# Weight sums added two pieces behind their loads, weights moved to multiples of 512 bytes, and four sigmoids spread out, in a decoder layer on Trainium2

## The chip, the cores and the metric

The kernel runs as one program on one core of a Trainium2 chip. The metric is the device time of one launch in microseconds (us); less is better. All times below are of that kind or come from one profiled execution of the same program.

The engines are named as in the profile: PE is the matrix engine (PEld is its loading of weights), DVE the vector engine, ACT the scalar engine, POOL the general one, SP the engine whose queue issues nearly all transfers. Each engine works through its own instructions in the order of the program.

## The reference

One decoder layer, in float32, for a sequence of S = 256 tokens of width D = 2048 (two blocks of 128 rows). Three kinds of attention read the same normalised input, gates mix them, and a gated feed-forward part follows:

```python
h = rms_norm(x, g_mix)
fq, fk, fv, f_logit, sq, sk, sv, mq, gates = split(h @ w_in)      # 6 + 6 + 4 heads of 128
o_fox = forgetting_attention(rms(fq), rms(fk), fv, cumsum(log_sigmoid(f_logit + b_forget)))
o_sb  = stick_breaking_attention(sq, sk, sv)
mk, mv = split(rms_norm(mem, g_mem) @ w_mem_kv)
o_mem = memory_attention(rms(mq), rms(mk), mv)
g = sigmoid(gates + b_gate)                                       # three gates, 2048 wide each
x = x + (g0*(o_fox @ w_br_fox) + g1*(o_sb @ w_br_sb) + g2*(o_mem @ w_br_mem)) @ w_out
u = causal_depthwise_conv(rms_norm(x, g_ffn) @ w_up)              # w_up is 2048 x 11264
x = x + (silu(u_gate) * u_val) @ w_down                           # w_down is 5632 x 2048
```

## The kernel before, in words

**Products.** Every float32 operand is split into a part `hi` and a rest `lo`, and each product is three passes: hi by hi, lo by hi, hi by lo (`three`, L284 to L286, and `passes`). Activations are the stationary operand ("weights" of PE), the model's matrices are the moving one, up to 512 columns at a time. `product` walks over the rows of a matrix in pieces of two blocks of 128 rows: a 512 KB load into one of four buffers `raw` (L140, on SP), a copy to `hi` on ACT (L141), a subtraction to `lo` on DVE (L142), both with four buffers, and then 12 matmuls. After each piece it calls `tick()`.

**Seven products for eight.** For parts of the gates, for the output projection and for the down projection, `blocked` replaces some groups of eight block products by seven. This needs sums of blocks of the matrix (`t_g`, `raw_t_d` and so on) and sums of blocks of the activations: `xs` for x (made by `x_sums`), `ms` for the merged heads, `sf` for the feed-forward part. In a gate's plan, such as "esesesee", "s" is a group of seven and "e" one of eight; four gates are done by such plans, with three "s" each.

**Weight sums ahead of time.** For the output and down projections the sums of the matrix are made in the background while the earlier stages run, and are kept in DRAM. `weight_sums` (L243 to L272) is a generator that `tick()` steps once. For one half of a sum it issues two loads of 256 KB (`pre`, L258), three additions on DVE (L265 to L267), and, `store` ticks after the loads, a store of 512 KB (`kept`, L270). After `period` ticks the next half begins. There is one buffer `pre`, so that a load has to wait for the store before it to land. While the first stages run, `period` is 4 and `store` is 3; from the third gate on (once "heads" is in `issued`) the period is 8. What is left at "merged" is done in the feed-forward stage by two further such generators with other buffers. There are 58 halves, 14 of `w_out` and 44 of `w_down`.

**Heads.** The attention heads are generators too, queued by `later` and stepped by `tick()`, at most two at a time: while PE does the projection of the next stage, it does the heads of the one before in between. `fox_head` has its PE work at L820 to L822 (`fa`, `fb`) and L724, after DVE copies at L815 and L837 (`fx`); stick-breaking heads are around L880 to L900.

**Order.** PE, DVE, ACT and SP instructions of the products, sums and loads are held in program order. The stages follow each other as: memory keys and values, memory queries, the fox projections f0 to f4, the stick-breaking projections s0 to s4, gates, branches, output projection, up, down.

**First sigmoids.** The first two gates are made by `product` while the last heads run. Their four sigmoids (two per gate, 128x1024 each) are issued together in `ready`, at the first blocked gate (L984), when the heads are done.

**Addresses.** Tiles of the pools are laid out one after the other in a partition's memory. In the kernel before, `ident` and `xs` stand 384 bytes past a multiple of 512; `xT`, `hi`, `lo`, `raw`, `pre` and nearly all other large tiles stand 32 bytes past one.

Of the kernel before, what the change touches and what calls it, by code (L numbers as in the profile page):

```python
# [9 lines left out]
F32 = mybir.dt.float32  # L10
F32R = mybir.dt.float32r
AF = mybir.ActivationFunctionType
# [3 lines left out]
P = 128  # L16
S = 256
NT = S // P
# [23 lines left out]
def hybrid_block(  # L42
# [25 lines left out]
    nc = tc.nc  # L68
    nc.scalar.preload_act_table_set("natural_log_exp_and_others")

    cst = ctx.enter_context(tc.tile_pool(name="cst", bufs=1))
    wp = ctx.enter_context(tc.tile_pool(name="wp", bufs=WBUFS))
    xt_pool = ctx.enter_context(tc.tile_pool(name="xt_pool", bufs=1))
    sm = ctx.enter_context(tc.tile_pool(name="sm", bufs=4))
    idle = cst.tile([P, 384], mybir.dt.bfloat16, name="idle")
    nc.vector.memset(idle, 0.0)
    sm_pad = sm.tile([P, 160], F32, tag="pad", bufs=1, name="sm_pad")
    nc.gpsimd.memset(sm_pad, 0.0)
# [2 lines left out]
    def bank(name):  # L81
        return pp.tile([P, 512], F32, tag="bank", name=name)
# [3 lines left out]
    spare = bank("spare")  # L86

    def keep_busy(n):
        for _ in range(n):
            tc.keep_in_program_order(  # L90
                nc.tensor.matmul(spare[:, :384], lhsT=idle[:, :P], rhs=idle, start=True, stop=True)
            )


# [2 lines left out]
    def later(gen):  # L97
        waiting.append(gen)
# [24 lines left out]
    def finish():  # L123
        while waiting or active:
            tick(beside=False)
# [104 lines left out]
    in_order = tc.keep_in_program_order  # L230
# [9 lines left out]
        for h in range(2)  # L240
    )

    def weight_sums(staging, period, store, end=None, delay=0, slower=0):  # L243


        for _ in range(delay):
            yield
        while halves and end not in issued:
            name, wv, nb, pr, h = halves.popleft()
            at = f"{name}{nb}_{pr}"  # L250
            if h == 0:
                sums_of[name, nb, pr] = dram.tile([P, 4, 512], F32, tag=f"kept_{at}", name=f"kept_{at}")
            kept = sums_of[name, nb, pr]
            w = staging(f"pre_{at}_{h}").rearrange("p (i c) -> p i c", i=4)
            n0 = nb * PIECE + h * 256
            for n in range(2):
                in_order(
                    nc.sync.dma_start(  # L258
                        w.rearrange("p (k n) c -> p k n c", k=2)[:, :, n],
                        wv[:, 2 * pr : 2 * pr + 2, n0 + n * 512 : n0 + n * 512 + 256],  # L260
                    )
                )

            both = w[:, 1:2].to_broadcast([P, 2, 256])
            in_order(nc.vector.tensor_tensor(w[:, 0:2], w[:, 0:4:3], both, ALU.add))  # L265
            in_order(nc.vector.tensor_tensor(w[:, T2], w[:, T1], w[:, T2], ALU.add))
            in_order(nc.vector.tensor_tensor(w[:, T4], w[:, T2], w[:, T4], ALU.add))  # L267
            for _ in range(store):
                yield
            in_order(nc.sync.dma_start(kept[:, :, h * 256 : (h + 1) * 256], w))  # L270
            for _ in range(period - store + (slower if "heads" in issued else 0)):
                yield  # L272
# [206 lines left out]
    nc.gpsimd.affine_select(  # L479
        after_r, ones, pattern=[[-1, P]], compare_op=ALU.is_gt, fill=0.0, base=0, channel_multiplier=1  # L480
    )
    qscale = cst.tile([P, 1], F32, name="qscale")
    nc.vector.memset(qscale, SCALE)

    keep_busy(7)
# [61 lines left out]
        nc.vector.tensor_reduce(tot, ss, AX.X, ALU.add)  # L547
        rsqrt_mean(dst, tot, NT, D, name)

    rstd = cst.tile([P, NT], F32, name="rstd")  # L550
    rstd_m = cst.tile([P, NT], F32, name="rstd_m")
    rstd_f = cst.tile([P, NT], F32, name="rstd_f")
    ssm = cst.tile([P, NT, 4], F32, name="ssm")
    ssx = cst.tile([P, NT, 4], F32, name="ssx")
    ssf = cst.tile([P, NT, 4], F32, name="ssf")

    rneg = cst.tile([P, NT], F32, name="rneg")

    mix = ctx.enter_context(ExitStack())
    op = mix.enter_context(tc.tile_pool(name="op", bufs=1))  # L560
# [1 line left out]
    gp = mix.enter_context(tc.tile_pool(name="gp", bufs=3))  # L562

    def block(name, dt=F32):
        return bp.tile([P, 1024], dt, tag="blk", name=name)
# [4 lines left out]
    def rows_of(b):  # L570
        return b.rearrange("p (t n) -> p t n", t=NT)
# [85 lines left out]
    def kv_tiles(k):  # L657
        return [
            wp.tile([P, PIECE], dt, tag=tag, bufs=n, name=f"{tag}_kv{k}")
            for tag, dt, n in (("raw", F32, WBUFS), ("hi", F32R, SBUFS), ("lo", F32R, SBUFS))  # L660
        ]

    tiles = kv_tiles(0)
# [56 lines left out]
    def weighted(pT, v, h, oh, o):  # L720
# [7 lines left out]

    ps = proj(C_MQ, MEM_W, "mq")
    background.append(  # L730
        weight_sums(lambda name: gp.tile([P, 1024], F32, tag="pre", bufs=1, name=name), 4, 3, "merged", slower=4)
    )
    finish()
    qm = heads_of(block("qm"))
# [204 lines left out]
    def merged_sums():  # L939
        yield 1  # L940
        for p in range(o_plans[0].count("s")):
            ms[p] = block(f"ms_{p}", F32R).rearrange("p (f l q) -> p f l q", f=4, l=2)
            pair_sums(mT[p], block(f"mw_{p}"), [(ms[p], slice(0, 4))])
            yield 3

    raw_g = lambda name: wp.tile([P, PIECE], F32, tag="raw", name=name)

    ordered[0] = True
    for m in range(2):
        gate = []  # L950
        for b, plan in enumerate(g_plans[m]):
            g, bias = [], []

            def biases(m=m, b=b, bias=bias):
                for n in (2 * m, 2 * m + 1):
                    bias.append(gp.tile([P, 512], F32, tag="bg", name=f"bg_{n}_{b}"))
                    nc.sync.dma_start(bias[-1], b_gate[0, b, n * 512 : (n + 1) * 512].partition_broadcast(P))

            def gathered(n0, Y, m=m, b=b, g=g, bias=bias):

                w = block(f"gw_{m}_{b}")
                g += [rows_of(block(f"g_{m}_{b}_{n}")) for n in range(2)]
                e, f = w[:, :512], w[:, 512:]
                scaled = lambda dst, src, c, n: nc.vector.scalar_tensor_tensor(
                    dst, src, c, bias[n], ALU.mult, ALU.add
                )
                nc.scalar.copy(e, Y[0])
                scaled(g[0][:, 0], Y[0], rstd[:, 0:1], 0)
                nc.vector.tensor_tensor(e, e, Y[1], ALU.add)
                yield  # L970
                nc.vector.tensor_tensor(f, e, Y[2], ALU.add)
                scaled(g[1][:, 0], f, rneg[:, 0:1], 1)
                nc.vector.tensor_tensor(f, e, Y[3], ALU.add)
                scaled(g[0][:, 1], f, rstd[:, 1:2], 0)
                yield
                nc.vector.tensor_tensor(f, f, Y[2], ALU.add)
                scaled(g[1][:, 1], f, rneg[:, 1:2], 1)

            def ready():
                finish()  # L980
                if "heads" not in issued:
                    issued.add("heads")
                    for v in gate[0] + gate[1]:
                        in_order(nc.scalar.activation(v, v, AF.Sigmoid))  # L984
                biases()

            def scaled_sums(n, ps, add):
                for t in range(NT):
                    nc.vector.scalar_tensor_tensor(g[n][:, t], ps[t], rstd[:, t : t + 1], add[t], ALU.mult, ALU.add)

            c0 = C_GATE + b * D + m * PIECE
            gate.append(g)
            if not plan:
                biases()
                for n in range(2):
                    ps = proj(c0 + n * 512, 512, f"g{n}_{b}")
                    g.append(rows_of(block(f"g_{m}_{b}_{n}")))
                    scaled_sums(n, ps, [bias[n]] * NT)
                continue
            X = blocked(  # L1000
                "g", w_in, f"{m}{b}", c0, plan, lambda p, j: xT(2 * p + j), lambda p, f: xs[:, p, f], raw_g, block,
                gathered, ready,
            )
            for n in range(2):
                scaled_sums(n, [X[t][n] for t in range(NT)], [g[n][:, t] for t in range(NT)])
                nc.scalar.activation(g[n], g[n], AF.Sigmoid)
        if m == 1:
            later(merged_sums())
        for n in range(2):
            acc = gate[branches[0][3]][n]  # L1010
            for i, (w, k0, nk, b) in enumerate(branches):
                ps = product(lambda k: oT[:, k0 + k], w[0], nk, (2 * m + n) * 512, 512, f"b{2 * m + n}_{b}")
                if (m, n, i) == (1, 0, 1):
                    xres = cst.tile([P, NT, D], F32, tag="xres", name="xres_again")
                    for t in range(NT):
                        nc.sync.dma_start(xres[:, t], xv[:, t])
                for t in range(NT):
                    g = gate[b][n]
                    if i == 0:
                        nc.vector.tensor_tensor(acc[:, t], g[:, t], ps[t], ALU.mult)  # L1020
                    else:
                        nc.vector.tensor_tensor(g[:, t], g[:, t], ps[t], ALU.mult)
                        nc.vector.tensor_tensor(acc[:, t], acc[:, t], g[:, t], ALU.add)
            later(merged_T(acc, 2 * m + n))
# [221 lines left out]
```

## Time and profile before

| | |
|---|---|
| time before, median of 3 runs | 1474.8 us (1473.0 to 1476.14) |
| profiled execution, its own time | 1474.81 us |
| its span in the trace | 1473.1 us |
| PE busy | 1462.5 us, 99% of the span |
| DVE busy | 1190.8 us, 81% |
| ACT busy | 838.6 us, 57% |
| moved by DMA | 369.42 MB, mean 251 GB/s |

The page gives for each engine the time that it was busy. The other views used below are the list of waits (which engine stood idle before which instruction, and for what: total, number of times, the longest), the timeline (start, duration, engine, line, operation, and in brackets the idle time before it and what ended it), the table of windows (busy time of each engine within a stretch), the groups of like instructions (count, busy time, mean ns of one) and the list of transfers (size and median time from issue to landing). A matmul's duration in the timeline overlaps with that of the next: the distance of their starts is what each costs.

### The profile page before, as it was taken

How to read it: one execution, taken by the hardware profiler on the slowest of the kernel's cores; microseconds unless marked ns; L12 is line 12 of the kernel's file. 1: busy time of each engine (PE TensorE's matmuls, PEld its weight loads, DVE VectorE, ACT ScalarE, POOL GpSimd, SP SyncE). 2: the span in 40 equal slices, each digit the busy share in tenths (PEclk: the TensorE clock that was granted, in tenths of full speed). 3: DMA queues.
4: the chain of work that ended last, by engine and by line, in shares of the span. 5: the costliest groups of instructions: out<-in, count | busy, mean ns of one | idle time of the engine just before them, and what ended most of it. 6: DMA issues, size and time to landing. Idle time of an engine off the chain costs nothing.

```text
span 1473.1 us, 20668 instructions
## 1 busy us (share of the span) xinstructions
PE 1462.5 (99%) x7337; PEld 1234.5 (84%) x7337; DVE 1190.8 (81%) x1818; ACT 838.6 (57%) x1194; POOL 17.1 (1%) x46
## 2 busy tenths in 40 slices
PE   9999999999999999999999999999999999999998
PEld 7888887888878888888888888888888888888887
DVE  5777667877689899997888899887778777997877
ACT  6755444464364455545666556565566565674664
POOL 0000000011000000000000000000000000000000
PEclk9999999999999999999999999999999999999999
DMA  9696797777878778887768898886766666797896
GB/s 311 200 302 216 234 298 257 235 249 247 288 262 281 222 242 264 273 311 234 260 189 269 287 294 278 282 261 184 200 187 186 199 184 203 240 323 272 257 327 222
DMA packets 205526, 369.42 MB, mean 251 GB/s; under 512 B 13530, under 2 KB 82030, under 8 KB 205166
## 3 DMA queue, kind: packets, MB, share of 16 engines
q1 hardware_dynamic: 204094, 365.99, 77.7%
q10 hardware_dynamic: 1328, 2.11, 0.4%
q8 instruction: 57, 0.93, 0.3%
q14 instruction: 47, 0.39, 0.1%
HBM read 335.54 MB, written 32.51 MB: 250 GB/s over the span
## 4 chain that ended last, share of the span: by engine, by line
PE 93%; DMA 3%; DVE 2%; ACT 1%; issue 1%; SPq 0%; POOL 0%; DVEq 0%; ACTq 0%; POOLq 0%
PE u L1149 22%; PE u L1150 11%; PE xd L286 4%; PE xd L285 4%; PE xd L284 4%; PE xg L286 3%; PE xg L285 3%; PE xg L284 3%; PE f L286 2%; PE f L285 2%; PE f L284 2%; PE b L286 2%; PE b L284 2%; PE b L285 2%; PE g L284 2%; PE g L286 2%
## 5 line engine op out<-in xcount | busy, mean ns | idle before, releaser
L1149 PE MATMUL u<-hT,hi_u 128*128 128x512 f32 x1232 | 428.5, 394 | 0.0
L1150 PE MATMUL u<-hT,lo_u 128*128 128x256 f32 x1232 | 341.4, 277 | 0.0
L142 DVE TENSOR_TENSOR lo_u<-raw_u,hi_u 128x1024 fp32r<-128x1024 f32 x176 | 215.1, 1222 | 85.0 <-ACT hi_u L141 84.3
L1149 PEld LDWEIGHTS u<-hT,hi_u 128*128 128x128 f32 x1232 | 231.0, 187 | 53.5
L141 ACT CAST hi_u<-raw_u 128x1024 fp32r<-128x1024 f32 x176 | 184.6, 1049 | 135.9 <-PE u L1149 115.2
L1150 PEld LDWEIGHTS u<-hT,lo_u 128*128 128x128 f32 x1232 | 231.4, 188 | 0.0
L279 DVE TENSOR_TENSOR lo_d<-raw_d,hi_d 128x1024 fp32r<-128x1024 f32 x88 | 106.7, 1222 | 20.5 <-ACT hi_d L278 17.8
L278 ACT CAST hi_d<-raw_d 128x1024 fp32r<-128x1024 f32 x88 | 91.9, 1054 | 47.9 <-PE xd L285 20.5
L278 ACT CAST hi_g<-raw_g 128x1024 fp32r<-128x1024 f32 (+1 forms) x64 | 62.1, 972 | 38.3 <-DMA raw_g<-in_w_in_dram 9.5
L279 DVE TENSOR_TENSOR lo_g<-raw_g,hi_g 128x1024 fp32r<-128x1024 f32 (+1 forms) x64 | 71.2, 1117 | 0.0
L141 ACT CAST hi_f<-raw_f 128x1024 fp32r<-128x1024 f32 (+1 forms) x40 | 38.6, 967 | 52.5 <-PE f L285 43.5
L284 PE MATMUL xd<-hi_d,aT 128*128 128x512 f32 x170 | 66.1, 389 | 0.0
L285 PE MATMUL xd<-hi_d,aT 128*128 128x512 f32 x170 | 66.1, 389 | 0.0
L286 PE MATMUL xd<-lo_d,aT 128*128 128x512 f32 x170 | 66.1, 389 | 0.0
L141 ACT CAST hi_s<-raw_s 128x1024 fp32r<-128x1024 f32 (+1 forms) x40 | 38.4, 961 | 41.8 <-PE s L285 25.8
L1149 PE MATMUL u<-hT_rest,hi_u 128*128 128x512 f32 x176 | 62.1, 393 | 0.0
L141 ACT CAST hi_b<-raw_b 128x1024 fp32r<-128x1024 f32 x32 | 33.7, 1052 | 42.8 <-PE b L285 17.8
L1121 ACT ACTIVATE y<-u,taps 128x256 f32<-128x256 f32 x88 | 49.2, 595 | 14.9 <-DVE u L1118 14.9
L142 DVE TENSOR_TENSOR lo_s<-raw_s,hi_s 128x1024 fp32r<-128x1024 f32 (+1 forms) x40 | 44.4, 1115 | 14.9 <-ACT hi_s L141 14.6
L286 PE MATMUL xg<-lo_g,xT 128*128 128x512 f32 x140 | 54.8, 391 | 0.4 <-DVE lo_g L279 0.4
L142 DVE TENSOR_TENSOR lo_f<-raw_f,hi_f 128x1024 fp32r<-128x1024 f32 (+1 forms) x40 | 44.3, 1116 | 13.1 <-ACT hi_f L141 11.5
L284 PE MATMUL xg<-hi_g,xT 128*128 128x512 f32 x140 | 54.5, 389 | 0.0
(482 smaller groups left out, 3490.7 us busy)
## 6 DMA issues: line engine op xcount, KB each, us to landing
raw_u<-in_w_up_dram SPq DMA_DIRECT2D x176, 512.0 KB, 4.7
raw_g<-in_w_in_dram SPq DMA_DIRECT2D x96, 512.0 KB, 4.6
raw_d<-in_w_down_dram SPq DMA_DIRECT2D x66, 512.0 KB, 5.4
pre_d<-in_w_down_dram SPq DMA_DIRECT2D x88, 256.0 KB, 4.8
kept_d<-pre_d SPq DMA_DIRECT2D x44, 512.0 KB, 5.2
raw_f<-in_w_in_dram SPq DMA_DIRECT2D x32, 512.0 KB, 5.4
raw_s<-in_w_in_dram SPq DMA_DIRECT2D x32, 512.0 KB, 5.1
raw_o<-in_w_out_dram SPq DMA_DIRECT2D x25, 512.0 KB, 6.2
```

Source lines behind the costliest of these rows:

```text
L141: pin(nc.scalar.copy(hi[:, :m], raw[:, :m]))
L142: pin(nc.vector.tensor_tensor(lo[:, :m], raw[:, :m], hi[:, :m].bitcast(F32), ALU.subtract))
L278: nc.scalar.copy(hi[:, :n], src)
L279: nc.vector.tensor_tensor(lo[:, :n], src, hi[:, :n].bitcast(F32), ALU.subtract)
L284: fix(nc.tensor.matmul(o, lhsT=ah, rhs=w[0], start=first, stop=False))
L285: fix(nc.tensor.matmul(o, lhsT=al, rhs=w[0], start=False, stop=False))
L286: fix(nc.tensor.matmul(o, lhsT=ah, rhs=w[1], start=False, stop=last))
L1121: nc.scalar.activation(y, u[:, 2:], AF.Identity, scale=tap(2), bias=tap(3))
L1149: nc.tensor.matmul(ps[i], lhsT=hi[:, j, c], rhs=hT(k + j), start=first, stop=False)
L1150: nc.tensor.matmul(ps[i][:, :S], lhsT=lo[:, j, c], rhs=hT(k + j)[:, :S], start=False, stop=last)
```

## The change

`weight_sums` gets a parameter `add`: the three additions are issued `add` ticks behind the loads instead of right behind them. The call for the first stages changes from period 4 and store 3 to period 5, store 4 and add 2, and `slower` from 4 to 3, so that the period after "heads" stays 8. The calls in the feed-forward stage keep `add` 0. With the longer period fewer halves are done before the feed-forward stage: 23 of the 58 are left to it instead of 18.

The four first sigmoids become a generator, `sigmoids`, that is queued by `later` and issues one sigmoid per tick.

Three tiles change their size or place: `idle` grows from 768 to 896 bytes per partition (the matmuls that use it still take 384 columns), `qscale` is padded to 416 bytes, and `rstd` and `rneg` become the two halves of one tile `rpair`. By this `xs` and `ident` move to multiples of 512 bytes, and the tiles that stood 32 bytes past a multiple of 512 move to multiples of 512 as well.

```diff
-    idle = cst.tile([P, 384], mybir.dt.bfloat16, name="idle")
+    idle = cst.tile([P, 448], mybir.dt.bfloat16, name="idle")
...
-                nc.tensor.matmul(spare[:, :384], lhsT=idle[:, :P], rhs=idle, start=True, stop=True)
+                nc.tensor.matmul(spare[:, :384], lhsT=idle[:, :P], rhs=idle[:, :384], start=True, stop=True)
...
-    def weight_sums(staging, period, store, end=None, delay=0, slower=0):
+    def weight_sums(staging, period, store, end=None, delay=0, slower=0, add=0):
...
+            for _ in range(add):
+                yield
             both = w[:, 1:2].to_broadcast([P, 2, 256])
             in_order(nc.vector.tensor_tensor(w[:, 0:2], w[:, 0:4:3], both, ALU.add))
             in_order(nc.vector.tensor_tensor(w[:, T2], w[:, T1], w[:, T2], ALU.add))
             in_order(nc.vector.tensor_tensor(w[:, T4], w[:, T2], w[:, T4], ALU.add))
-            for _ in range(store):
+            for _ in range(store - add):
                 yield
             in_order(nc.sync.dma_start(kept[:, :, h * 256 : (h + 1) * 256], w))
             for _ in range(period - store + (slower if "heads" in issued else 0)):
...
-    qscale = cst.tile([P, 1], F32, name="qscale")
+    qscale = cst.tile([P, 104], F32, name="qscale")[:, :1]
...
-    rstd = cst.tile([P, NT], F32, name="rstd")
+    rpair = cst.tile([P, 2, NT], F32, name="rpair")
+    rstd, rneg = rpair[:, 0], rpair[:, 1]
...
-    rneg = cst.tile([P, NT], F32, name="rneg")
...
-        weight_sums(lambda name: gp.tile([P, 1024], F32, tag="pre", bufs=1, name=name), 4, 3, "merged", slower=4)
+        weight_sums(lambda name: gp.tile([P, 1024], F32, tag="pre", bufs=1, name=name), 5, 4, "merged", slower=3, add=2)
...
+    def sigmoids(tiles):
+        for v in tiles:
+            in_order(nc.scalar.activation(v, v, AF.Sigmoid))
+            yield
...
-                    for v in gate[0] + gate[1]:
-                        in_order(nc.scalar.activation(v, v, AF.Sigmoid))
+                    later(sigmoids(gate[0] + gate[1]))
```

## The prediction

> **What bounds the kernel now.** I began with the page: its span, the busy times and the chain that ended last.
>
> ```profile
> span 1473.1 us, 20668 instructions
> PE 1462.5 (99%) x7337; PEld 1234.5 (84%) x7337; DVE 1190.8 (81%) x1818; ACT 838.6 (57%) x1194; POOL 17.1 (1%) x46
> PE 93%; DMA 3%; DVE 2%; ACT 1%; issue 1%; SPq 0%; POOL 0%; DVEq 0%; ACTq 0%; POOLq 0%
> ```
>
> PE is the bound: 10.6 us of the span are not PE. The number of matmuls stays as it is, so this change can gain only where PE stands idle or where one matmul costs more than its like. The profiled execution took 1474.81 us, 1.7 us more than its span and equal to the median of the runs (1474.8), so sums are made against 1474.8. About 0.2%, 2.95 us, can be told from no change.
>
> Next, PE's waits (line, whom it waited for, us in total, times, the longest):
>
> ```profile
> PE fa L724 <- DVE fx L837: 1.8, 2, 1.3
> PE xg L286 <- DVE lo_t_g L279: 1.6, 1, 1.6
> PE fa L820 <- DVE fx L815: 1.0, 1, 1.0
> PE xg L286 <- DVE lo_g L279: 0.4, 2, 0.2
> ```
>
> They are single events. Where they lie and how much each really costs is told by PE's timeline, by the distance of the starts:
>
> ```profile
> 206.70 0.39 PE L286 MATMUL s<-lo_s,xT 128*128 128x512 f32 x1
> 208.11 0.41 PE L820 MATMUL fa<-ident,fx 128*128 128x128 f32 x2 [1.02 <-DVE fx L815]
> 223.68 0.39 PE L286 MATMUL s<-lo_s,xT 128*128 128x512 f32 x1
> 225.41 0.70 PE L724 MATMUL fa<-fx,vf 128*128 128x256 f32 x2 [1.34 <-DVE fx L837]
> 249.03 0.70 PE L724 MATMUL fa<-fx,vf 128*128 128x256 f32 x2 [0.44 <-DVE fx L837]
> 420.75 0.50 PE L286 MATMUL xg<-lo_t_g,xT 128*128 128x512 f32 x1 [1.61 <-DVE lo_t_g L279]
> ```
>
> Three lie in the fox heads (A at 208, B at 225, C at 249), one at the start of the first blocked gate (E at 421). DVE's timeline shows what held DVE before B, C and E:
>
> ```profile
> 223.74 0.69 DVE L265 TENSOR_TENSOR pre_o<-pre_o 128x512 f32<-128x512 f32 x1 [1.59 <-DMA pre_o<-in_w_out_dram]
> 224.81 0.55 DVE L837 COPY fx<-fb 128x384 f32<-128x384 f32 x1
> 243.69 0.69 DVE L265 TENSOR_TENSOR pre_d<-pre_d 128x512 f32<-128x512 f32 x1 [1.32 <-DMA pre_d<-in_w_down_dram]
> 407.38 0.69 DVE L265 TENSOR_TENSOR pre_d<-pre_d 128x512 f32<-128x512 f32 x1 [2.68 <-DMA pre_d<-in_w_down_dram]
> 418.87 0.69 DVE L393 TENSOR_TENSOR t_g<-raw_g 128x512 f32<-128x512 f32 x1 [1.72 <-DMA raw_g<-in_w_in_dram]
> ```
>
> At B the copy `fx` that PE wants stands behind an addition that waited for its own load. At C the addition's wait came 5 us earlier and left DVE late. At E two things meet: an addition waited 2.68 us, and `raw_g` came late. SP issues `raw_g` only when DVE frees a buffer, and DVE follows ACT, which was busy with this:
>
> ```profile
> 406.00 1.28 ACT L984 ACT_TABLE_LOAD   x1
> 407.29 2.96 ACT L984 ACTIVATE g<-g 128x1024 f32<-128x1024 f32 x3
> 410.53 0.63 ACT L278 CAST hi_g<-raw_g 128x512 fp32r<-128x512 f32 x1 [0.28 <-DMA raw_g<-in_w_in_dram]
> ```
>
> **The additions.** In all, DVE and SP wait for these sums as follows; below it, their transfers, with the median us to landing:
>
> ```profile
> DVE pre_d L265 <- DMA pre_d<-in_w_down_dram: 26.3, 10, 4.3
> DVE pre_o L265 <- DMA pre_o<-in_w_out_dram: 16.7, 8, 3.7
> SPq L258 <- DMA kept_d<-pre_d: 38.8, 26, 4.4
> SPq L270 <- DVE pre_d L267: 24.8, 21, 2.2
> pre_o<-in_w_out_dram SPq DMA_DIRECT2D x28, 256.0 KB, 3.5
> pre_d<-in_w_down_dram SPq DMA_DIRECT2D x88, 256.0 KB, 4.8
> kept_d<-pre_d SPq DMA_DIRECT2D x44, 512.0 KB, 5.2
> raw_s<-in_w_in_dram SPq DMA_DIRECT2D x32, 512.0 KB, 5.1
> ```
>
> A full piece is 12 matmuls; at 0.227 us (the window below) that is 2.72 us. Two ticks are 5.4 us, more than either landing of `pre`, so the waits of 16.7 and 26.3 us should largely go from DVE. But "behind" is counted in program order, and SP's place against DVE's is the scheduler's. In the order of instructions of before, the load stands on SP on average 1.5 pieces later than the additions stand on DVE between f4 and s4 (a load behind piece s2_6, its additions behind s2_0); in the changed order it is 0.8 (pre_o1_1_0 behind s1_12, added behind s1_8; but pre_o0_3_1 behind f4_10 on both). From the third gate on the additions stand one or two pieces after the load instead of level with it. So in the gates the relief is whole, in the heads about half.
>
> The terms. A: 208.11 − 206.70 − 0.23 = 1.18; its idle is 1.02, so a restart adds 0.16. B: 225.41 − 223.68 − 0.23 = 1.50. C: 0.44 + 0.16 = 0.60. E: 1.61 + 0.16 = 1.77. Together 5.05. A has no addition right ahead of it: there a late `raw_s` held DVE, so it goes only by the loads falling at other places. Nothing in the trace shows which stall the new places bring. Its bounds are 0 and all of A, B and C, 3.28, if the same loads meet the same heads again; a gain isn't to be had there, since PE can't be less than not idle. I take 1.5, the price of B, since half the relief in the heads leaves about one such meeting. The two waits of 0.2 us for `lo_g` (L279) I leave as they are: there PE waits for the cast and subtraction of a piece, which the change doesn't move.
>
> Period 5 for 4 leaves five more halves to the feed-forward stage. They cost nothing there while PE is covered:
>
> ```profile
> 720.00:1240.00 520.00, 520.00 (x2960) 453.45 (x2960) 419.19 (x698) 312.85 (x478) 0.00 (x0) 1.00 0.75 229
> L265 DVE TENSOR_TENSOR pre_d<-pre_d 128x512 f32<-128x512 f32 x44 | 30.2, 686 | 26.4 <-DMA pre_d<-in_w_down_dram 26.3
> L266 DVE TENSOR_TENSOR pre_d<-pre_d 128x256 f32<-128x256 f32 x44 | 18.7, 424 | 0.8
> L267 DVE TENSOR_TENSOR pre_d<-pre_d 128x256 f32<-128x256 f32 x44 | 18.6, 423 | 0.8
> ```
>
> PE is busy all 520 us of it (columns: PE, PEld, DVE, ACT, POOL, then the clock, DMA share, GB/s). A half is 0.69 + 0.42 + 0.42 = 1.53 us of DVE: five are 7.7 us, and DVE has 101 us free. Their 5 MB are 4% on 119 MB, at a DMA share of 0.75. Without the cover at most those 7.7 us would show.
>
> **The sigmoids.** One sigmoid is 2.96/3 = 0.99 us. In the changed order one table load and one sigmoid stand in a row, then a `hi` or two before each of the other three; so the casts at 410.53 come up to 1.97 us earlier, more than E's 1.77. No table load is added. The gates that these sigmoids finish are read only when the branches are mixed, far later. E goes by either cause; I count it whole.
>
> **The addresses.** Matmuls whose weights are `xs` can be compared with like ones whose weights are `xT`, eight blocks against seven in one gate:
>
> ```profile
> 508.99:514.43 5.44, 5.44 (x25) 4.50 (x24) 5.32 (x8) 2.08 (x2) 0.00 (x0) 1.00 0.94 318
> 514.43:519.30 4.87, 4.87 (x22) 3.94 (x21) 3.76 (x4) 3.71 (x5) 0.00 (x0) 1.00 0.59 190
> 515.79 0.39 PE L284 MATMUL xg<-hi_g,xs 128*128 128x512 f32 x1
> 516.50 0.40 PE L284 MATMUL yg<-hi_t_g,xs 128*128 128x512 f32 x1
> ```
>
> Twenty-four by `xT` take 5.44, 226.7 ns each, without idle; the 21 of a group of seven would take 4.76 and took 4.87. Three starts by `xs` lie 0.71 apart, 237 ns each. Weights at 384 past a multiple of 512 and moving data at 32 cost 0.11 us more per seven. Twelve sevens of gates: 1.3 us. After the change both stand at 0, as `xT` and its moving data stand at the same residue now, so I take the 226.7 row. The bounds are 0 (the excess isn't the address) and 1.3 from these rows. For all other matmuls both operands move together and I take nothing; no row shows residue 0, so a change of either sign per matmul can't be excluded, and 1 ns on 7337 would be 7.3 us.
>
> The Trainium skill ("TensorE: Matmul & The Clock Gate", section "Back-to-back issue gap") gives the warm distance as columns/2.4 plus about 2.5 ns, with no term for addresses. For 512 columns that is an estimate of 216 ns; the trace has 227 and 237 at a granted clock of 1.00, so here the measurement has a part that the rule lacks. By that rule the addresses would bring nothing, and the sum would be 1.3 us higher.
>
> The sum: 1474.8 − 5.05 − 1.3 + 1.5 = **1470.0 us**.
>
> **Rivals.** *The addresses bring nothing*: 1471.3, in which the rest of the forecast stands (3 in 10 within it). *The stalls only move*: SP still can't load `pre` before `kept` has landed (38.8 us, 26 times), so `raw_s` is late in the heads as at A, and the other heads meet additions. All 5.05 come back and only the addresses count: 1473.5. For it speaks that A has no addition at its head, and the order's half relief; against it, that E has two causes and both are relieved. *Slower: the later store starves the loads.* Count from the `lo` after which the additions run: additions 1.53, landing of the store 5.2, two load issues 0.9 (517.52 in SP's timeline, quoted next), next `raw` 5.1: 12.7 us.
>
> ```profile
> 213.30 0.53 SPq L270 DMA_DIRECT2D kept_o<-pre_o  x1
> 217.52 0.88 SPq L258 DMA_DIRECT2D pre_o<-in_w_out_dram  x2
> ```
>
> That `raw` was wanted five pieces later before (13.6 us, less a wait of 43.0/18 = 2.4 where there was one) and four after (10.9): 0.9 early to 1.5 late before, 1.8 late after. It decides wherever ACT and DVE are less than 1.8 us ahead of PE. From 197 to 406 there are 15 periods of five ticks; if half of them lose 1.8, that is 13.5, and with B, C, E and the addresses gained (5.2) the time is 1483.1. Against it: four buffers each of `hi` and `lo`, up to three pieces of lead, and longest DVE waits of 4.3 us that mostly don't reach PE.
>
> **Chances.** The forecast, with or without the addresses, 0.70; matmuls at residue 0 cheaper throughout 0.03 (about 1463); the stalls only move 0.15; starved loads 0.12. Hence faster 0.73, same 0.15, slower 0.12. The range goes down to 1467.0 (no new stall, 1468.5, and a little of the cheaper matmuls) and up to 1475.5, which takes in the moved stalls and the mildest starving.
>
> **What would show it.** Right: no idle PE before `fa` with DVE at L265; the wait of 1.6 at L279 gone; the waits at L265 below 15 us in all; a seven of the gates in 4.76 us; PE busy all through the feed-forward stage. Wrong: new rows of idle PE behind `lo_s` or `lo_g` with ACT waiting for `raw`, SP's wait at L270 well over 24.8; sevens still at 4.87; or a plain product's matmuls at other than 227 ns.

## The result, and the profile after

The changed kernel takes 1483.1 us (median of 20 runs; 19 of them 1480.4 to 1486.1, one 1472.8) against 1475.15 us before (20 runs): a ratio of 1.0052, 95% interval 1.0041 to 1.0063. It is slower by some 8 us. Its profiled execution took 1481.42 us.

The page after, span, busy times and the chain that ended last:

```profile
span 1479.7 us, 20666 instructions
PE 1470.7 (99%) x7337; PEld 1238.4 (84%) x7337; DVE 1192.9 (81%) x1818; ACT 839.5 (57%) x1194; POOL 18.6 (1%) x46
PE 90%; DVE 5%; DMA 3%; issue 1%; ACT 1%; POOL 0%; SPq 0%; DVEq 0%; ACTq 0%; POOLq 0%
```

The span grew by 6.6 us and PE's busy time by 8.2, with the same 7337 matmuls. So the idle time went down, as forecast, and the matmuls became dearer. The waits of PE show the first:

```profile
PE b L288 <- DVE lo_b L142: 1.3, 2, 0.7
PE xg L288 <- DVE lo_g L281: 1.2, 3, 0.6
...
PE fa L725 <- DVE fx L838: 0.2, 1, 0.2
```

The fox heads' 2.8 us of idle PE are down to 0.2, the 1.6 us for `lo_t_g` are gone, new waits stand before `b`, and those before `xg` have grown (0.4 before). The groups of the up stage show the second; first before, then after (count, busy us, mean ns):

```profile
L1149 PE MATMUL u<-hT,hi_u 128*128 128x512 f32 x1232 | 428.5, 394 | 0.0
L1150 PE MATMUL u<-hT,lo_u 128*128 128x256 f32 x1232 | 341.4, 277 | 0.0
```

```profile
L1154 PE MATMUL u<-hT,hi_u 128*128 128x512 f32 x1232 | 436.2, 399 | 0.0
L1155 PE MATMUL u<-hT,lo_u 128*128 128x256 f32 x1232 | 345.9, 281 | 0.0
```

Here the model's matrix is the stationary operand, and a matmul of 512 columns (by `hi_u`) alternates with one of 256 (by `lo_u`). Windows tell their real cost (us, PE busy and its count, then the other engines). Before, then after:

```profile
780.00:1240.00 460.00, 460.00 (x2655) 402.27 (x2655) 372.37 (x633) 272.75 (x417) 0.00 (x0) 1.00 0.76 232
```

```profile
780.00:1240.00 460.00, 460.00 (x2606) 398.99 (x2605) 375.64 (x642) 268.70 (x410) 0.00 (x0) 1.00 0.78 239
```

In the same 460 us PE did 49 matmuls fewer, without idle and at the same clock. A pair costs 460/2655 x 2 = 346.5 ns before and 353.0 after; by the starts in the trace it is 346.7 and 353.3. The stage has 1408 pairs, and the 1344 behind 778 us pay the difference: 9.0 us. That is the loss, and it isn't spread at random but a rhythm. In PE's timeline, of before and then of after, take the starts of the rows by `hi_u`: in the rows shown they lie 0.35, 0.34 and 0.35 us apart before, and 0.35, 0.36 and 0.35 after:

```profile
900.11 0.40 PE L1149 MATMUL u<-hT,hi_u 128*128 128x512 f32 x1
900.34 0.28 PE L1150 MATMUL u<-hT,lo_u 128*128 128x256 f32 x1
900.46 0.39 PE L1149 MATMUL u<-hT,hi_u 128*128 128x512 f32 x1
900.69 0.27 PE L1150 MATMUL u<-hT,lo_u 128*128 128x256 f32 x1
900.80 0.40 PE L1149 MATMUL u<-hT,hi_u 128*128 128x512 f32 x1
901.03 0.28 PE L1150 MATMUL u<-hT,lo_u 128*128 128x256 f32 x1
901.15 0.39 PE L1149 MATMUL u<-hT,hi_u 128*128 128x512 f32 x1
```

```profile
900.05 0.40 PE L1154 MATMUL u<-hT,hi_u 128*128 128x512 f32 x1
900.28 0.28 PE L1155 MATMUL u<-hT,lo_u 128*128 128x256 f32 x1
900.40 0.40 PE L1154 MATMUL u<-hT,hi_u 128*128 128x512 f32 x1
900.64 0.28 PE L1155 MATMUL u<-hT,lo_u 128*128 128x256 f32 x1
900.76 0.40 PE L1154 MATMUL u<-hT,hi_u 128*128 128x512 f32 x1
901.00 0.28 PE L1155 MATMUL u<-hT,lo_u 128*128 128x256 f32 x1
901.11 0.40 PE L1154 MATMUL u<-hT,hi_u 128*128 128x512 f32 x1
```

By the first rows of the stages, the up stage began at 752.13 us for 754.51 and the down stage at 1251.26 for 1244.69: in these two executions 2.4 us had been gained by then, and the up stage lost 9.0.

### The profile page after: what moved, and what is told of

It is laid out like the page before. It is cut to its first block, busy times and chain, and to the rows that moved or that the text cites. A ratio compares the mean times of both kernels' runs of the same rounds, so it can differ in the third digit from the quotient of the medians.

```text
span 1479.7 us, 20666 instructions
## 1 busy us (share of the span) xinstructions
PE 1470.7 (99%) x7337; PEld 1238.4 (84%) x7337; DVE 1192.9 (81%) x1818; ACT 839.5 (57%) x1194; POOL 18.6 (1%) x46
## 4 chain that ended last, share of the span: by engine, by line
PE 90%; DVE 5%; DMA 3%; issue 1%; ACT 1%; POOL 0%; SPq 0%; DVEq 0%; ACTq 0%; POOLq 0%
PE u L1154 22%; PE u L1155 11%; PE xd L287 4%; PE xd L286 4%; PE xd L288 4%; PE f L288 2%; PE f L286 2%; PE f L287 2%; PE s L286 2%; PE s L288 2%; PE s L287 2%; PE xg L288 2%; PE g L286 2%; PE g L288 2%; PE g L287 2%; PE xg L286 2%
## 5 line engine op out<-in xcount | busy, mean ns | idle before, releaser
L1154 PE MATMUL u<-hT,hi_u 128*128 128x512 f32 x1232 | 436.2, 399 | 0.0
L1155 PE MATMUL u<-hT,lo_u 128*128 128x256 f32 x1232 | 345.9, 281 | 0.0
L142 DVE TENSOR_TENSOR lo_g<-raw_g,hi_g 128x1024 fp32r<-128x1024 f32 x32 | 39.2, 1229 | 21.1 <-ACT hi_g L141 20.8
```

The costliest lines, as they stand in the source:

```text
L142: pin(nc.vector.tensor_tensor(lo[:, :m], raw[:, :m], hi[:, :m].bitcast(F32), ALU.subtract))
L1154: nc.tensor.matmul(ps[i], lhsT=hi[:, j, c], rhs=hT(k + j), start=first, stop=False)
L1155: nc.tensor.matmul(ps[i][:, :S], lhsT=lo[:, j, c], rhs=hT(k + j)[:, :S], start=False, stop=last)
```

## The experiments

**Addresses or transfers?** Two things in the change reach the up stage: every operand stands elsewhere, and five more halves of weight sums are loaded there. The first run makes the three size edits alone on the kernel before, the second takes them back from the changed kernel.

```diff
# e1, on the kernel before
-    idle = cst.tile([P, 384], ...)            +    idle = cst.tile([P, 448], ...)
-    qscale = cst.tile([P, 1], ...)            +    qscale = cst.tile([P, 104], ...)[:, :1]
-    rstd, rneg: two tiles                     +    rpair = cst.tile([P, 2, NT], ...)
# e2, on the changed kernel: the same three lines the other way
```

> The kernel before with the address edits alone (the three tiles' sizes); no edit of the sums or the sigmoids. Theory A, the addresses cost: in the feed-forward up stage each pair of matmuls (512 and 256 columns) takes 353.3 ns instead of 346.7, 1408 pairs, +9.3 us, and the sevens of the gates gain 1.3 at most: 1475.1 + 8.0 = 1483.1 us, ratio 1.0054. Theory B, the five more halves of weight sums in the up stage slow PE through their transfers: pairs stay at 346.7 and the time is 1475.1 - 1.3 = 1473.8, ratio 0.999.

> The changed kernel with the addresses of before (sums two ticks behind, period 5, sigmoids one at a time stay). Theory A: pairs at 346.7 ns; the stalls that went less those that came in the trace of the changed kernel, about -1.9 us: 1473.2 us, ratio 0.9987. Theory B: pairs at 353, 1475.1 + 9.3 - 1.9 = 1482.5, ratio 1.005.

Measured: e1 1482.8 us, ratio 1.0050 (1.0032 to 1.0068); e2 1473.0, ratio 0.9983 (0.9971 to 0.9995). Windows of e1 and of e2:

```profile
780.00:1240.00 460.00, 460.00 (x2605) 398.85 (x2604) 369.95 (x629) 269.87 (x414) 0.00 (x0) 1.00 0.72 228
```

```profile
780.00:1240.00 460.00, 460.00 (x2655) 402.57 (x2655) 378.30 (x647) 271.80 (x414) 0.00 (x0) 1.00 0.76 243
```

The address edits cost the whole loss, and the transfers of five more halves cost PE nothing. The other two parts of the change are a small gain in e2, but none beside the addresses: e1 has 1.0050 without them, the changed kernel 1.0052 with them.

**Which address?** Four runs moved tiles by themselves, all with the new schedule.

```diff
# e3, on the changed kernel: all large tiles and xs at 32 past a multiple of 512
-    idle = cst.tile([P, 448], ...)            +    idle = cst.tile([P, 464], ...)
# e4, on the changed kernel: 32 bytes ahead of xT, hT, oT and aT
+    xt_pad = xt_pool.tile([P, 8], F32, tag="pad", name="xt_pad")
# e6, e7, on e2: all tiles 512, 256 bytes higher
-    idle = cst.tile([P, 384], ...)            +    idle = cst.tile([P, 640 or 512], ...)
# e8, on e2: only xT, hT, oT, aT 512 bytes higher
+    xt_pad = xt_pool.tile([P, 128], F32, tag="pad", name="xt_pad")
```

> The changed kernel with the tile idle 32 bytes larger, so that all large tiles and xs too stand 32 past a multiple of 512. Theory A in the form that residue 0 is the slow one: pairs at 346.7, sevens at 226.7 per matmul as well, 1473.2 - 1.3 = 1471.9 us, ratio 0.998. If only unequal residues of xs and xT mattered and something else slows the up stage (theory B): 1482 to 1483.

> The changed kernel with 32 bytes put ahead of xT, hT, oT and aT: hi and lo stay at 0 past a multiple of 512, xT and hT go to 32. Which operand matters? If the weights' place does (hi_u, lo_u in the up stage): pairs stay at 353.3, about 1483; and plain products (weights xT now at 32, moving hi at 0) stay at 226.7. If the moving operand's place does: pairs 346.7, about 1475. If unequal places cost, as for the sevens of before (384 against 32, 234 ns): the plain products slow too, up to 7 ns on some 4500 matmuls, over 1500 us.

> The schedule of the run without address edits, all tiles 512 bytes higher (hi and hT 544 past a multiple of 1024 instead of 32, xs still 384 past a multiple of 512). If the place modulo 1024 decides the up stage: pairs at 353.3 ns, about 1482 us, although every residue modulo 512 is that of before. If only the residue modulo 512 or the place of xs does: 346.7, about 1473.

> The same, all tiles 256 bytes higher (hi and hT 288 past a multiple of 1024). Modulo 1024 with two halves: 346.7, about 1473. Modulo 512 with 32 as a lucky place: 353 or another value.

> The same as the run without address edits, but only the tiles from xT and hT on 512 bytes higher; hi and lo stay. If hT's place modulo 1024 decides: pairs 353.3, about 1482. If hi's and lo's (the weights of the up stage): 346.7, about 1473. Plain products: both operands still at 32 modulo 512, 226.7 expected.

e3 missed: 1482.0 us, ratio 1.0042 (1.0028 to 1.0057), pairs at 353, although `hi` and `hT` stand at 32 as before. So residue 0 isn't the slow one. e6, e7 and e8 (one run each) took 1472.7, 1473.5 and 1475.9 us with pairs at 346.7: the place of `hi` and `hT` modulo 1024 isn't it either. In e4 the plain products slowed (its groups):

```profile
L1156 PE MATMUL u<-hT,hi_u 128*128 128x512 f32 x1232 | 428.3, 390 | 0.0
L1157 PE MATMUL u<-hT,lo_u 128*128 128x256 f32 x1232 | 347.7, 282 | 0.0
...
L288 PE MATMUL xd<-hi_d,aT 128*128 128x512 f32 x170 | 67.3, 396 | 0.0
```

Both operands of `xd` now stand 32 bytes apart: 396 ns by the profile (389 before), and from start to start 233.3 ns for 226.7. That is the price of unequal places that the sevens paid before, now paid by nearly all plain matmuls of 512 columns; the run took 1491.0 us. The up stage, though, kept its 346.7 ns (window of e4):

```profile
780.00:1240.00 460.00, 460.00 (x2657) 408.29 (x2656) 380.48 (x655) 275.02 (x420) 0.00 (x0) 1.00 0.76 244
```

**xs, ident, or the up stage's own operands?** The slow kernels had one thing in common, so far: xs and ident had moved. Here they move by themselves (e5), then xs without ident (e9), by where a small tile is put; a few small constants, which no matmul of the up stage reads, move along.

```diff
# on e2: gmix_c (160 bytes) is placed right behind idle (e5), or behind ident (e9)
+    gmix_c = cst.tile([P, 2 * KT + 4], F32, name="gmix_c")
...
-    gmix_c = cst.tile([P, 2 * KT + 4], F32, name="gmix_c")
```

> The new schedule (sums two ticks behind, sigmoids spread) with every tile from hi on at the byte where the kernel before has it; only xs and ident move, from 384 to 32 past a multiple of 512, by a small tile placed ahead of them. If the up stage depends only on where hi and hT stand: pairs stay at 346.7 ns as in the run without the address edits; and if the sevens depend only on xs standing at the same residue as the moving data: 226.7 per matmul instead of 234, 144 matmuls, -1.1 us. 1473.0 - 1.1 = 1471.9 us, ratio 0.9975. If xs's place made the up stage slow (the rival, since the three slow kernels all had xs moved): 1481 to 1483.

> As the run in which xs and ident both moved to 32 past a multiple of 512, except that ident stays at 384, where the kernel before has it; xs alone is moved. Theory C, PE's pairs in the up stage have two rhythms, 346.7 and 353.3 ns, and the two transposes of rp at about 777 us (moving operand: ident) set which one holds for the rest of the stage: 346.7 ns, and with the sevens at 226.7 per matmul 1473.0 - 1.1 = 1471.9 us, ratio 0.9975. Theory D, the place of xs itself (which holds the residual x in the up stage) slows it: 353.3 and 1482 to 1483.

The rival of e5 holds: 1482.8 us, ratio 1.0048 (1.0034 to 1.0061), with every operand of the up stage where it was. e9: 1481.4, ratio 1.0058 (1.0045 to 1.0071). Moving xs is enough, and the up stage's pairs don't touch xs. Its place by itself doesn't decide, though: in e4 and e7 xs and ident had moved too, and the pairs stayed at 346.7. Its slot, however, then holds the residual x, which 16 transposes turn into the last part of `hT` at about 760 us, and 778 us brings two more transposes, of `rp`. I followed the pairs from start to start. In before, after, e3, e5 and e9 the stage begins with 353 ns a pair. After the transposes of `hT` it is 346.7 in before, after, e3 and e5, but 353.3 in e9. After those of `rp` it stays 346.7 in before and goes to 353.3 in after, e3 and e5. Nothing else changes it until the stage ends.

**Is it a rhythm that one matmul can change?**

```diff
# e10, on the changed kernel, right behind the two transposes of rp
+            nc.tensor.matmul(rp[:, S : S + P], lhsT=rb[:, 0], rhs=upto, start=True, stop=True)
```

> The changed kernel with one more matmul of 128 columns right after the two transposes of rp, its moving operand upto, 32 past a multiple of 64 where ident is at 0; its result is not used. Theory C: this one matmul, some 0.2 to 0.5 us, changes the rhythm for the following 470 us from 353.3 to 346.7 ns a pair: 1483.1 - 9 = 1474 us, ratio 0.999. Theory D, or any theory by which the addresses of the up stage's own operands decide: 353.3 and 1483.4.

> The changed kernel with one matmul after rp once more. By its span and by the sum of pairs at 346.7 ns, sevens at 227 and the new stalls: 1473.4 us, ratio 0.999, with pairs at 346.7 again if the rhythm follows from the order and the addresses and not from chance.

Yes: 1473.4 us, ratio 0.9997 (0.9988 to 1.0006), and in a second set 1472.5, ratio 0.9991 (0.9982 to 1.0000). In e10's timeline the added matmul is the second row; the window behind it is that of the rest of the stage:

```profile
777.52 0.38 PE L1050 MATMUL rp<-ident,rb 128*128 128x128 f32 x2
777.73 0.39 PE L1051 MATMUL rp<-upto,rb 128*128 128x128 f32 x2
777.88 0.47 PE L1155 MATMUL u<-hT,hi_u 128*128 128x512 f32 x1
```

```profile
780.00:1240.00 460.00, 460.00 (x2656) 405.71 (x2655) 378.48 (x649) 273.28 (x417) 0.00 (x0) 1.00 0.76 243
```

A single matmul of the program (two instructions of PE, 7339 for 7337), 0.15 us from its start to the next, gains 9 us, with all operands of the stage where the changed kernel has them.

**Does the place of rb set it?** My rule then was that transposes whose operands stand at equal places modulo 64 change the rhythm. Moving `rb` by 32 bytes, with nothing else changed, tests it on three kernels.

```diff
-            rb = junk("rb")[:, :S].rearrange(...)
+            rb = junk("rb")[:, 8 : 8 + S].rearrange(...)
```

> The kernel before, with rb (the weights of the two transposes of rp) 32 bytes further in its tile; every instruction and every other address stays. Theory C in its last form: transposes whose operands stand at the same place modulo 64 change the rhythm of the pairs, those at different places leave it. rb then stands at 0 modulo 64 like ident, so the fast rhythm of before is lost at 778 us: 353.3 ns a pair, 1474.6 + 9.3 = 1483.9 us, ratio 1.006. Theory D, the places of xs and of the up stage's own operands decide: 346.7 and 1474.6.

> The changed kernel with rb 32 bytes further, nothing else. Theory C: the operands of rp no longer stand at the same place modulo 64, so the fast rhythm that holds after the transposes of hT stays: 346.7 ns, and with the sevens fast 1472 to 1473 us, ratio 0.998. Theory D: 353.3 and 1482 to 1483.

> The kernel with xs at 32 and ident at 384, which was slow from the transposes of hT on, with rb 32 bytes further. Theory C: rb and ident now stand at the same place modulo 64, which changes the rhythm, this time from slow to fast: 353.3 up to 776 us and 346.7 from there, about 1472.5 us, ratio 0.998. Theory D, or a theory that equal places make the pairs slow: 353.3 throughout, 1482.

All three went against it: 1474.3 us on before (ratio 0.9997, 0.9985 to 1.0008), 1482.0 on after (1.0045), 1483.1 on e9 (1.0064), each with the rhythm that it had without the move. The rule is dropped. What is left is that the transposes end one rhythm and another follows, which one depending on the rhythm before and on the place of xs and ident.

The traces show two things more, read off afterwards and tested by no run.

- The starts are recorded to the nanosecond, and by them 346.7 ns is the mean of two rhythms: starts 347, 347 and 346 ns apart in turn, or 350 and then 343 or 344. The slow rhythm is 350, 350 and 360. After the transposes of `hT`, before, e2, e6 to e8 and e11 to e13 have the first, and after, e1, e3, e5 and e14 the second. In all of these the two transposes of `rp` turn the first into the second, and the second into the slow one. So the kernels part at the transposes of `hT`, where their pairs still cost the same, and those of `rp` bring it out. e10, e16 and e17 have the second too, and behind `rp` and the added matmul they have the first. In e4 the first holds throughout; e9 and e15 are slow both before and after `rp`.
- In the sixteen kernels without e10's matmul the pairs end up slow where xs stands as many bytes past a multiple of 64 as `hT` (after, e1, e3, e5, e9, e14, e15), and fast where it stands 32 bytes off.

**The other two parts.** Each alone on the kernel before:

```diff
# e11: add=0 as a parameter of weight_sums, the additions behind "for _ in range(add): yield"
-  ..., 4, 3, "merged", slower=4)       +  ..., 5, 4, "merged", slower=3, add=2)
# e12: the generator sigmoids, and in ready
-  for v in gate[0] + gate[1]: ...      +  later(sigmoids(gate[0] + gate[1]))
```

> The kernel before with the edit of the weight sums alone (two ticks behind, period 5). If the sums cause the stalls in the fox heads: the idle times before fa at 208, 225 and 249 us go (3.0 of 3.3), new ones of 0.7 to 0.8 come before b and xg, and the wait of 1.6 us at the first blocked gate goes if the additions were its cause, and stays if the sigmoids were. 1475 - 2.0 = 1473 us in the first case, 1474.6 in the second; pairs of the up stage at 346.7.

> The kernel before with the sigmoids one at a time, nothing else. If they cause the wait at the first blocked gate: the 1.6 us go, the heads' stalls stay, 1475 - 1.8 = 1473.2 us. If the additions cause it: 1475. Pairs of the up stage at 346.7.

e11: 1474.7 us, ratio 1.0000 (0.9991 to 1.0010); e12: 1474.8, ratio 1.0005 (0.9995 to 1.0016). PE's waits in e11, then in e12:

```profile
PE xg L288 <- DVE lo_g L281: 1.4, 3, 0.8
...
PE b L288 <- DVE lo_b L142: 0.8, 2, 0.6
PE yo L288 <- DVE lo_o L281: 0.5, 1, 0.5
```

```profile
PE yg L286 <- DVE lo_t_g L279: 1.2, 1, 1.2
...
PE xg L286 <- DVE lo_g L279: 1.0, 3, 0.6
PE fa L724 <- DVE fx L837: 0.6, 1, 0.6
```

The sums alone end the waits in the heads and at the first blocked gate, and bring others before `xg`, `b` and `yo`; the 2 us expected of it don't show in the time. The sigmoids alone leave the wait at the first blocked gate (1.2, now at `yg`): the additions, with their period, were its cause. The other profiles agree. All with the additions of before (e1 and e13 too) have a wait of 1.2 to 1.8 us there, and none with the later ones has more than 0.5. And e12 tells more. Up to that gate it is the same program as before, instruction by instruction, yet its heads lost 0.6 us for 2.8. The stalls that I read as three fixed events differ from one execution to the next.

**Do the late stores starve the branches?** In after, ACT waited longer for the loads `raw_b` of one branch (first row, from the waits; 9.9 us before). Then SP's timeline ahead of one of PE's two waits for `b`, at 663 us, and ACT's row:

```profile
ACT hi_b L141 <- DMA raw_b<-in_w_br_sb_dram: 16.0, 6, 4.1
```

```profile
644.64 0.53 SPq L272 DMA_DIRECT2D kept_d<-pre_d  x1
646.97 0.38 SPq L140 DMA_DIRECT2D raw_b<-in_w_br_sb_dram  x1
650.43 0.88 SPq L258 DMA_DIRECT2D pre_d<-in_w_down_dram  x2
651.42 0.40 SPq L140 DMA_DIRECT2D raw_b<-in_w_br_sb_dram  x1
```

```profile
657.73 1.05 ACT L141 CAST hi_b<-raw_b 128x1024 fp32r<-128x1024 f32 x1 [4.13 <-DMA raw_b<-in_w_br_sb_dram]
```

The second `raw_b` stands behind the loads of `pre`, which wait for the store to land, and was issued 4.5 us after the first; ACT then waited 4.13; PE's wait behind it cost 0.7, from start to start. In e16, on e10, the store comes two ticks later from the third gate on:

```diff
-            for _ in range(store - add):
+            for _ in range(store - add + (2 if add and "heads" in issued else 0)):
...
-  ..., 5, 4, "merged", slower=3, add=2)       +  ..., 5, 4, "merged", slower=1, add=2)
```

> The run with one matmul after rp, and from the third gate on the store of a half comes six ticks behind its loads instead of four (period 8 as before). If SP's hold at the store starves raw_b: the stalls before b and yo (2.0 to 2.9 us together in the profile of its base) go, 1473.4 - 2 = 1471.4 us, ratio 0.9975. If it is the landing of the store ahead of the next load, or the traffic of the branches itself: they stay or move, 1473.4.

1472.4 us, ratio 0.9989 (0.9980 to 0.9998); its base in the same set (e17) 1472.5, 0.9991. In its profile the waits before `b` and `xg` are 0.8 and 0.6 us, where e17's had 1.2 and 0.8 and another 0.2 before `yo`, but the times don't tell the two apart, and the 2 us expected didn't come. e2 and e16 beat both kernels, by 0.2 and 0.1%; the intervals of e10 and e17, which are the same kernel, reach or pass 1.

## Why the prediction was wrong

The forecast was 1470.0 us, range 1467.0 to 1475.5; the time is 1483.1. The step that failed is the one on the addresses: "For all other matmuls both operands move together and I take nothing". The bound stood beside it (1 ns on 7337 matmuls would be 7.3 us, of either sign), and I gave it 0.03, on the faster side alone. It was worth +9.0 us, in one stage. I had read the up stage's window for its idle time (none) and its DMA share, and not for its cost per matmul, so that nothing in the prediction spoke of its rhythm.

- *The sevens.* Right. `yg` by `xs` went from 397 to 391 ns in the profile, as here in after, and from 233.5 to 227.7 ns from start to start:

```profile
L286 PE MATMUL yg<-hi_t_g,xs 128*128 128x512 f32 x36 | 14.1, 391 | 0.0
```

  The 144 matmuls by `xs` and the 36 by `xT` that stand among them gained 6 ns each: 1.0 us, near the 1.3 of the sum. The 36 show that the cost isn't a matter of one matmul's own operands: theirs stand at equal places in before, and they cost 234 there as well. The Trainium skill ("TensorE: Matmul & The Clock Gate", "Back-to-back issue gap") gives its warm gap of columns/2.4 + 2.5 ns for an isolated matmul and without a term for addresses. That gives an estimate of 216 ns for 512 columns. The traces differ from it: one behind the other, the plain matmuls cost 226.7 ns, and the same ones 233.3 in e4.
- *The stalls.* The direction was right in the profile, and the size was not. DVE's waits for `pre`, 43.0 us before, are 6.0 after (the row below and 1.8 for `pre_o`), well under the 15 that I had named. The stalls A, B, C and E of 5.05 us gave way, from start to start, to 0.37 in the heads and 3.3 before `b` and `xg`, where 0.7 had stood. But 5.05 was one execution's draw: in three further profiles with the additions of before (e1, e12, e13) the heads lost 0.7 to 0.95 us, not 3.3. What e2 shows for sums and sigmoids together is -2.5 us by its ratio, interval -4.3 to -0.7, against the -3.55 that the sum had. The other runs show less: 0.0 (-1.3 to 1.5) for the sums alone, 0.7 (-0.7 to 2.4) for the sigmoids alone, and after is no faster than e1. So the size of this gain, and whether there is one, stays open.

```profile
DVE pre_d L267 <- DMA pre_d<-in_w_down_dram: 4.2, 3, 2.8
```

- *E.* I gave it two causes. e11 and e12 show one: the additions.
- *The feed-forward stage.* Five more halves at no cost: right, by e2 (2655 matmuls in the window, as before).
- *The rivals.* The slower one named 1483.1 us, which is the time measured. That is chance, for its reason didn't hold: a load behind the later store cost PE 0.7 us at one place, not 13.5 over the heads, where PE's waits are lower than before, and SP's wait of 24.8 us ahead of the store of `pre_d` fell to 18.6. (The 517.52 in its sum is a slip for 217.52, the row shown; the sum is not touched.)

What stays open is why the pairs have these rhythms, and how the place of xs and ident picks one. The runs show that it does (e1, e2, e5, e9), that it is picked at the transposes, and that one matmul changes it (e10, e17); not the rule by which. One of after's 20 runs took 1472.8 us, and one of e3's ten 1475.4; no profile of those runs tells whether they had the other rhythm.

## What to carry to other kernels

A stage in which PE is always busy is not thereby at its best: divide its window by its matmuls and look at the starts before taking it as fixed, above all where matmuls of two lengths alternate. An edit that moves tiles touches every matmul, so bound it by the longest stage and on both sides. And a stall seen in one profile is one draw; price it by several executions, or by half.

## What the runs showed of the hardware

- Plain matmuls of 512 columns, one behind the other, cost 226.7 ns from start to start where weights and moving data stand a multiple of 512 bytes apart, and 233.3 where they stand 32 bytes off that (e4), or 352 (`xs` in the sevens of before, 233.5). Both at 32 is as good as both at 0 (e3). Neighbours count too: the 36 of the sevens of before with both at 32 cost 234. Whether a smaller step than 512 would do wasn't tried.
- Alternating matmuls of 512 and 256 columns run at 346.7 or 353.3 ns a pair, at the same addresses and clock (e10 and after differ by one matmul), depending on what interrupted them last. The rhythm then held for 470 us. Pairs with the same mean of 346.7 can be in two rhythms, which the same two transposes turn into different ones (before and after).
